# Hybrid decoder layer: the change-over between the two FFN products reordered, the last weight group loaded earlier, its last product split in two

## The chip, the cores and the metric

The kernel runs on one core of one Trainium2 chip. The metric is the time of one execution on the device in microseconds, the median of several runs. The engines are named as in the profile: PE (matrix products; PEld loads their stationary operand), DVE (vector), ACT (scalar), POOL (GpSimd) and SP (which issues DMAs).

## The reference

One decoder layer on x of 512 tokens by 2048. The token mixer (gated linear attention and differential attention) comes first and isn't touched here. The change lies in the second half, a gated MLP with a causal depthwise convolution, and its closing norm:

```python
h = rmsnorm(x, ffn_pre_norm)
up = h @ w_ffn_in                       # 2048 x (2 * 5632)
a, b = up[..., :D_FF], up[..., D_FF:]
a = conv_w[0] * a_pad[0:S] + conv_w[1] * a_pad[1:S+1] + conv_w[2] * a_pad[2:S+2] + conv_b
f = (gelu(a) * b) @ w_ffn_out           # 5632 x 2048
x = x + rmsnorm(f, ffn_post_norm)
```

## The kernel before

**Numbers and pieces.** Every fp32 operand is split into a high part (an ACT copy to the reduced fp32 type, L138 or L151) and a low part (a DVE subtraction, L139 or L152), and each product is three matmuls: high by high, high by low, low by high. A *weight half* ("granule", L129) is 128 x 1024 weights, loaded by DMA into a raw tile, split into one of three slots of the tile `ring`, or into a spare pair of tiles (`xhi`, `xlo`; from the pool tag "rt", or one pair that is kept).

**Units.** The 5632 hidden columns are 44 blocks of 128, 11 groups of four. Group 0 is done plainly (its result lies in DRAM as `ud0`); groups 1 to 10 go through a scheme of seven products instead of eight on 2 x 2 blocks (class `Unit`, L1221). A unit has the products `x0`, `z0`, `y0`, `z1`, `x1`, `y1`, `y2`, each of two weight halves, of which each takes 12 matmuls of 512 columns (down) or 24 of 256 (up). Products of one letter add up in the same PSUM banks; `x0` also opens `y`. After each product `out` reads the banks: ACT copies or DVE adds. The weights of a product are sums too: `x0` and `z1` are followed by an accumulating DMA that POOL issues (L1246, L1506) onto the raw tile, and DVE adds others (L1464, L1281). The other operand of a product (`a11`, `s5`, `s2`, `s3`, `a12`, `s7`, `a22`) is a token-block sum. For the up units it lies in `ah`, `al` and six tiles; for the down units it comes back from DRAM (`sd`) into a small tile `st` and is split into a fixed place of `ah`, `al` (`prepare`, L1389; places at L1384). Place (3, 1) belongs to no operand; (0, 0) is `a11`'s, free after the last `x0`. Small tiles (tag t4) have six buffers.

**Order.** The up units run first (20 of them, L1428), then ten down units, five pairs of groups by two halves of the 2048 output columns, each adding into `acc[t]`, one 128 x 2048 tile for each of four token tiles. Outside of blocks marked as ordered by hand, the kernel's planner orders the instructions by its own model of their times, and may move a load far ahead of its place in the text. Inside `manual_schedule(engines=IN_ORDER)` PE, ACT, DVE and POOL take the order of the text, while SP's DMAs are still placed by the planner.

**The change-over** (`change_over`, L1523) is such an ordered block: the last four products of the last up unit u (from `x1`), all of the first down unit d0 but for the end of `z` and `x`, and `x0` of d1, written as a list of products. `run_in_order` (L1487) splits weight halves two or three ahead of their product, and after each half calls the functions that `at` and `prepare_at` hung there: loads, operand splits, weight sums, the sums that u's result is stored as (`late_sums`), and the allocation of `acc` (`late_tiles`).

**The last group.** `whole` (L1670) loads the two halves of `ud0` and splits them into places (3, 1) and (0, 0). `last_group` (L1620) multiplies it by the last weights in four column blocks c of 512 for the four token tiles t: `ffn_out_part` is 12 matmuls and DVE's add into `acc` (L1608); `square` is ACT's sum of squares (L1613); `scale` multiplies by the gain (L1617); a DVE sum over the four blocks and two POOL steps (L145, L147) give the reciprocal root; `finish` is the final sum with the residual (L1637) and the store. Block 0 is ordered by the planner, blocks 1 to 3 by hand, token tile by token tile; block 3's weights are split after the first product of block 1.

Of the kernel before, what the change touches and what calls it, by code (L numbers as in the profile page):

```python
# [17 lines left out]
P = 128  # L18
# [17 lines left out]
def hybrid_layer(ctx: ExitStack, tc: tile.TileContext, x, attn_pre_norm, w_in, w_alpha_up, b_alpha,  # L36
# [10 lines left out]
    def dma(o, i):  # L47
        return nc.sync.dma_start(out=o, in_=i)
# [114 lines left out]
    def bcast_row(tile_ap, row):  # L163
        dma(tile_ap, row.partition_broadcast(P))
# [1224 lines left out]
    def prepare(c, n):  # L1389
        raw = small_tile("st")  # L1390
        dma(raw, sd[c][n].rearrange("p g x -> p (g x)"))
        split(piece(ah, *place[n]), piece(al, *place[n]), raw)
# [60 lines left out]
    def at(u, seg, g, *fs):  # L1453
        hooks.setdefault((u, seg, g), []).extend(fs)

    def load_unit(u):
        u.t = [load_t(u.block(0, 0, g), u.a) for g in range(2)]
        u.b22, u.b21 = [], []

    def load_b(u, name, i, j, by=None):  # L1460
        getattr(u, name).extend(load(u.block(i, j, g), u.a, by) for g in range(2))

    def add_t(u, name, g):
        tt(u.t[g], u.t[g], getattr(u, name)[g], ALU.add)  # L1464
# [13 lines left out]
    def prepare_at(c, n, load_at, split_at):  # L1478
        f, g = prepare_parts(c, n)
        at(*load_at, f)  # L1480
        at(*split_at, g)
# [40 lines left out]

    def change_over(u):  # L1523
        d0, d1 = downs[:2]
        order = [(u, "x1"), (d0, "x0"), (u, "y1"), (u, "y2")]
        order += [(d0, g) for g in ("z0", "y0", "z1", "x1")] + [(d1, "x0"), (d0, "y1"), (d0, "y2")]
        at(u, "x1", 1, late_tiles)
        prepare_at(0, "s2", (u, "x1", 0), (d0, "x0", 1))
        prepare_at(0, "s3", (u, "x1", 1), (u, "y1", 0))
        prepare_at(0, "s7", (u, "y1", 1), (u, "y2", 0))  # L1530
        prepare_at(0, "a12", (d0, "x0", 0), (d0, "z0", 0))
        prepare_at(0, "a22", (u, "y2", 0), (d0, "y0", 0))
        at(u, "x1", 1, lambda: (add_t(u, "b21", 0), add_t(u, "b21", 1)))
        at(u, "x1", 0, lambda: load_b(d0, "b22", 1, 1))
        at(u, "y1", 1, lambda: load_b(d0, "b21", 1, 0))
        at(d0, "z0", 1, lambda: load_unit(d1))
        for g in range(2):
            at(u, "y2", g, lambda g=g: add_t(d0, "b22", g))
        at(d0, "z1", 0, lambda: add_t(d0, "b21", 0))
        at(d0, "x1", 0, lambda: add_t(d0, "b21", 1))  # L1540
        for where in ((d0, "z0", 0), (d0, "y0", 0), (d0, "z1", 0), (d0, "x1", 0)):
            at(*where, lambda: late_sums.pop(0)())
        return order

# [5 lines left out]
        prepare(0, n)  # L1550
    with tc.manual_schedule(engines=IN_ORDER):
        run_in_order(order, lambda i: 2 if i < 10 else 3)

    extra[0] = True
    downs[1].z0(held=True)
    for i, u in enumerate(downs):
        if i == 0:
            continue
        nxt = downs[i + 1] if i + 1 < len(downs) else None
        nc_ = (i + 1) // 2  # L1560
        first = i % 2 == 0
        last_cb = i % 2 == 1 and nxt is not None

        if first:
            prepare(i // 2, "s3")
        if i == 6:
            g3 = large_tile("g3")
            bcast_row(g3, ffn_post_norm[0])
        u.y0()
        if first:  # L1570
            prepare(i // 2, "a12")
        if last_cb:
            prepare(nc_, "a11")
        u.z1()
        if first:
            prepare(i // 2, "s7")
        u.x1()
        if last_cb:
            prepare(nc_, "s5")
        if nxt is not None:  # L1580
            nxt.x0()
        if first:
            prepare(i // 2, "a22")
        u.y1()
        if last_cb:
            prepare(nc_, "s2")
        u.y2()
        if nxt is not None:
            nxt.z0()
# [2 lines left out]


    def ffn_out_weights(gi, c):
        return [granule(w_y3[:, 4 * gi + 2 * q:4 * gi + 2 * q + 2, 512 * c:512 * (c + 1)], 2,
                        spare={(3, 1): True, (2, 1): "rt", (3, 0): "rt"}.get((c, q))) for q in range(2)]

    def ffn_out_part(us, gr, t, c):
        b = bank()
# [17 lines left out]
        tt(acc[t][:, sl] if dst is None else dst, acc[t][:, sl], g3[:, sl], ALU.mult)  # L1617


    def last_group(gi, us):  # L1620
        gr = ffn_out_weights(gi, 0)
        for t in range(NT):
            ffn_out_part(us, gr, t, 0)
            square(t, 0)
            scale(t, 0)
        gr = {c: ffn_out_weights(gi, c) for c in (1, 2)}

        rs = {}
        x1 = {t: v[:, h].rearrange("p k c -> p (k c)").bitcast(F32)
              for t, (v, h) in enumerate(((ah, 1), (al, 1), (ah, 2), (al, 2)))}  # L1630
        for t in range(NT):
            dma(x1[t], x1d[t])

        def finish(t, *ps, last=None):
            for i in ps:
                sl = slice(512 * i, 512 * (i + 1))
                stt(acc[t][:, sl], last if last is not None and i == 3 else acc[t][:, sl], rs[t],  # L1637
                    x1[t][:, sl], ALU.mult, ALU.add)
                if t == 3:
                    dma(out2[t * P:(t + 1) * P, sl], acc[t][:, sl])  # L1640
                elif i % 2:
                    sl = slice(512 * i - 512, 512 * (i + 1))
                    dma(out2[t * P:(t + 1) * P, sl], acc[t][:, sl])

        with tc.manual_schedule(engines=IN_ORDER):
            end = small_tile("end")[:, :512]
            for t in range(NT):
                ffn_out_part(us, gr[1], t, 1)
                square(t, 1)
                if t == 0:  # L1650
                    gr[3] = ffn_out_weights(gi, 3)
                else:
                    finish(t - 1, 0)
                scale(t, 1)
                if t:
                    finish(t - 1, 1)
                ffn_out_part(us, gr[2], t, 2)
                square(t, 2)
                if t:
                    finish(t - 1, 2, 3)  # L1660
                ffn_out_part(us, gr[3], t, 3)
                square(t, 3)
                scale(t, 2)
                scale(t, 3, end if t == 3 else None)
                ss = small.tile([P, 1], F32, name="ss", tag="ss")
                nc.vector.reduce_sum(ss, ssf[t], axis=AX.X)
                rs[t] = rsqrt_mean(ss, D)
            finish(3, 0, 1, 2, 3, last=end)

    whole = []  # L1670
    for q, at in enumerate(((3, 1), (0, 0))):
        raw = small_tile("st")
        dma(raw, ud0[:, 2 * q:2 * q + 2, :].rearrange("p n t -> p (n t)"))
        hi, lo = (piece(v, *at) for v in (ah, al))
        split(hi, lo, raw)
        for n in range(2):
            whole.append((hi[:, S * n:S * (n + 1)], lo[:, S * n:S * (n + 1)]))
    last_group(0, whole)


# [28 lines left out]
```

## Time and profile before

| | |
|---|---|
| median of 3 runs | 2078.6 us (2077.53 to 2078.65) |
| the profiled execution | 2076.67 us, span 2075.0 us, granted PE clock 0.999 |
| PE busy | 2047.0 us, 99% |
| DVE busy | 1507.1 us, 73% |
| ACT busy | 1000.0 us, 48% |
| DMA | mean 173 GB/s |

Times inside the program are microseconds from the span's start. The up units end, and the change-over lies, about 1618 to 1660; the down units run to about 2022; the last group runs from there to the end, its last product ending near 2065. A busy PE row counts overlapping matmuls, so what a matmul costs is read from the distance of two starts. In a timeline row the bracket gives how long the engine was idle before the row, and what ended that.

### The profile page before, as it was taken

To read this page: it belongs to the slowest core of one execution; us is meant where nothing else is said; L and a number is where in the kernel's file an instruction comes from. 1 tells how busy PE (TensorE), PEld (TensorE's weight loads), DVE (VectorE), ACT (ScalarE), POOL (GpSimd) and SP (SyncE) were. 2 spreads that over 40 slices of the span, in tenths; PEclk is the share of its full clock that TensorE was granted. 3 is DMA by queue.
4 is the path that set the end of the run, shared out by engine and by line. 5 is a ranking of instruction groups with operands and counts; after the bars stand their busy time and mean duration, and the time that the engine had idled before them with its cause. 6 is when DMAs were issued, how large, how long until landed. Compare 5 with 4: busy or idle time off the path is not lost.

```text
span 2075.0 us, 35488 instructions
## 1 busy us (share of the span) xinstructions
PE 2047.0 (99%) x14417; PEld 1893.9 (91%) x14417; DVE 1507.1 (73%) x1790; ACT 1000.0 (48%) x1301; POOL 290.2 (14%) x306
## 2 busy tenths in 40 slices
PE   7999999999999999999999999999999999999998
PEld 6799999999988889899999999999999888888786
DVE  5967777666762265977777777777777888988877
ACT  5544444455652243454554554555455654444433
POOL 0112223222200000011011111111110111101100
PEclk9999999999999999999999999999999999999999
DMA  5488887878883354458667577567677896775753
GB/s 213 121 189 184 191 199 180 196 174 200 197 263 120 93 181 152 113 119 196 147 154 194 138 163 189 135 166 178 147 164 188 225 249 171 196 208 144 180 155 142
DMA packets 281465, 358.61 MB, mean 173 GB/s; under 512 B 14848, under 2 KB 223156, under 8 KB 279380
## 3 DMA queue, kind: packets, MB, share of 16 engines
q1 hardware_dynamic: 192148, 259.85, 37.3%
q0 software_dynamic: 84800, 94.38, 29.9%
q10 hardware_dynamic: 4352, 2.10, 0.4%
q8 instruction: 113, 1.85, 0.3%
q14 instruction: 52, 0.43, 0.1%
HBM read 311.72 MB, written 44.56 MB: 172 GB/s over the span
## 4 chain that ended last, share of the span: by engine, by line
PE 67%; DVE 2%; issue 1%; DMA 1%; ACT 1%; POOL 0%; DVEq 0%; POOLq 0%; SPq 0%; ACTq 0%
PE bank L1298 12%; PE bank L1299 12%; PE bank L1300 12%; PE bank L1401 6%; PE bank L1402 6%; PE bank L1400 6%; PE bank L194 3%; PE bank L193 3%; PE bank L192 3%; PE bank L176 1%; PE bank L175 1%; PE bank L174 1%; DVE ring L139 1%; PE bank L1605 0%; PE bank L1606 0%
## 5 line engine op out<-in xcount | busy, mean ns | idle before, releaser
L138 ACT ACTIVATE ring<-raw 128x1024 fp32r<-128x1024 f32 x316 | 334.7, 1061 | 494.0 <-PE bank L1299 115.6
L139 DVE TENSOR_TENSOR ring<-raw,ring 128x1024 fp32r<-128x1024 f32 x316 | 384.1, 1221 | 251.6 <-ACT ring L138 250.6
L1298 PE MATMUL bank<-ah,ring 128*128 128x256 f32 x1280 | 353.4, 276 | 1.5 <-DVE u L1331 1.5
L1300 PE MATMUL bank<-ah,ring 128*128 128x256 f32 x1280 | 353.3, 276 | 0.0
L1299 PE MATMUL bank<-al,ring 128*128 128x256 f32 x1280 | 353.3, 276 | 0.0
L138 ACT ACTIVATE ring<-rt 128x1024 fp32r<-128x1024 f32 x220 | 233.3, 1061 | 248.3 <-PE bank L1299 155.1
L139 DVE TENSOR_TENSOR ring<-rt,ring 128x1024 fp32r<-128x1024 f32 x220 | 268.5, 1222 | 90.1 <-ACT ring L138 87.1
L1298 PEld LDWEIGHTS bank<-ah,ring 128*128 128x128 f32 x1280 | 240.3, 188 | 1.7 <-ACT ring L138 1.7
L1299 PEld LDWEIGHTS bank<-al,ring 128*128 128x128 f32 x1280 | 240.3, 188 | 0.1
L1300 PEld LDWEIGHTS bank<-ah,ring 128*128 128x128 f32 x1280 | 240.3, 188 | 0.0
L1401 PE MATMUL bank<-ring,ah 128*128 128x512 f32 x424 | 165.3, 390 | 1.9 <-DVE ring L139 1.9
L1402 PE MATMUL bank<-ring,al 128*128 128x512 f32 x424 | 165.0, 389 | 0.0
L1400 PE MATMUL bank<-ring,ah 128*128 128x512 f32 x424 | 152.4, 389 | 0.0
L193 PE MATMUL bank<-ring,ah 128*128 128x512 f32 x280 | 109.6, 393 | 0.0
L192 PE MATMUL bank<-ring,ah 128*128 128x512 f32 x280 | 109.4, 396 | 0.0
L194 PE MATMUL bank<-ring,al 128*128 128x512 f32 x280 | 108.9, 392 | 0.0
L1246 POOL DMA_DIRECT2D raw<-in_w_ffn_in_dram x40 | 51.2, 1309 | 395.3 <-DVE ring L139 395.3
L1401 PEld LDWEIGHTS bank<-ring,ah 128*128 128x128 f32 x424 | 79.6, 188 | 19.3 <-DVE ring L139 2.8
L1246 POOL DMA_DIRECT2D rt<-in_w_ffn_in_dram x40 | 50.9, 1279 | 327.0 <-DVE ring L139 315.0
L1400 PEld LDWEIGHTS bank<-ring,ah 128*128 128x128 f32 x424 | 79.6, 188 | 16.6
L1402 PEld LDWEIGHTS bank<-ring,al 128*128 128x128 f32 x424 | 79.6, 188 | 16.5
L797 PE MATMUL bank<-ring,ah 128*128 128x256 f32 x320 | 91.8, 287 | 0.2 <-ACT ah L151 0.2
(358 smaller groups left out, 5646.3 us busy)
## 6 DMA issues: line engine op xcount, KB each, us to landing
raw<-in_w_ffn_in_dram SPq DMA_DIRECT2D x96, 512.0 KB, 4.7
raw<-in_w_in_dram SPq DMA_DIRECT2D x56, 512.0 KB, 4.6
raw<-in_w_ffn_out_dram SPq DMA_DIRECT2D x48, 512.0 KB, 6.2
raw<-in_w_in_dram POOLq DMA_DIRECT2D x40, 512.0 KB, 7.3
rt<-in_w_ffn_in_dram SPq DMA_DIRECT2D x40, 512.0 KB, 5.9
rt<-in_w_ffn_in_dram POOLq DMA_DIRECT2D x40, 512.0 KB, 6.1
raw<-in_w_ffn_in_dram POOLq DMA_DIRECT2D x40, 512.0 KB, 6.6
raw<-in_w_o_dram SPq DMA_DIRECT2D x32, 512.0 KB, 4.1
```

The lines of the kernel that those rows point to most:

```text
L138: act(hi, raw, AF.Copy)
L139: tt(lo, raw, hi.bitcast(F32), ALU.subtract)
L192: mm(banks[t], ah[:, t, s, :], w[0][:, k, :], start=st, stop=False)
L193: mm(banks[t], ah[:, t, s, :], w[1][:, k, :], start=False, stop=False)
L194: mm(banks[t], al[:, t, s, :], w[0][:, k, :], start=False, stop=sp)
L1246: nc.gpsimd.dma_start(out=raws[g].rearrange("p (a b) -> p a b", a=self.a), in_=self.block(0, j, g), accum_op=ALU.add)
L1298: mm(o, wh, sh[:, :, kk, :], start=start and kk == 0 and n == 0, stop=False, **NOW)
L1299: mm(o, wh, sl[:, :, kk, :], start=False, stop=False, **NOW)
L1300: mm(o, wl, sh[:, :, kk, :], start=False, stop=kk == HK - 1, **NOW)
L1400: mm(b[j], sh[:, o:o + P], w[0][:, q, :], start=start and st == 0, stop=False, **NOW)
L1401: mm(b[j], sh[:, o:o + P], w[1][:, q, :], start=False, stop=False, **NOW)
L1402: mm(b[j], sl[:, o:o + P], w[0][:, q, :], start=False, stop=st == 3, **NOW)
```

## The change

1. In the change-over the list opens with `x0` of d0, and the last up unit follows as `y1`, `x1`, `y2` (before: `x1`, `x0` of d0, `y1`, `y2`). The loads, splits, weight sums and late sums hang at other products, most of the splits and late sums later.
2. `ud0`'s two halves are loaded at the head of down unit 8 (`load_first`) and split behind the next unit's `x0` (`split_first`, the first half there, the second after the loop), in place of both after the loop.

3. In the last group, block 0 is ordered by hand too. Block 1's weights are loaded into "rt" tiles and split after block 0's first product (its second half into the kept pair); block 2's after block 0. Block 1's products for token tiles 0 and 1 come first, with block 3's weights split between them; then the order is as before.
4. The last product (token tile 3, block 3) becomes `last_block`: two halves of 256 columns on two banks, each with its add and square. DVE sums the first parts of the squares while the second half runs, and POOL takes the last add and the root. `scale` of block 2 moves ahead of it.

```diff
--- before.py
+++ after.py
@@ -1522,23 +1522,23 @@
 
     def change_over(u):
         d0, d1 = downs[:2]
-        order = [(u, "x1"), (d0, "x0"), (u, "y1"), (u, "y2")]
+        order = [(d0, "x0"), (u, "y1"), (u, "x1"), (u, "y2")]
         order += [(d0, g) for g in ("z0", "y0", "z1", "x1")] + [(d1, "x0"), (d0, "y1"), (d0, "y2")]
-        at(u, "x1", 1, late_tiles)
-        prepare_at(0, "s2", (u, "x1", 0), (d0, "x0", 1))
-        prepare_at(0, "s3", (u, "x1", 1), (u, "y1", 0))
-        prepare_at(0, "s7", (u, "y1", 1), (u, "y2", 0))
-        prepare_at(0, "a12", (d0, "x0", 0), (d0, "z0", 0))
-        prepare_at(0, "a22", (u, "y2", 0), (d0, "y0", 0))
-        at(u, "x1", 1, lambda: (add_t(u, "b21", 0), add_t(u, "b21", 1)))
-        at(u, "x1", 0, lambda: load_b(d0, "b22", 1, 1))
-        at(u, "y1", 1, lambda: load_b(d0, "b21", 1, 0))
+        at(d0, "x0", 0, lambda: load_b(d0, "b22", 1, 1))
+        at(d0, "x0", 0, late_tiles)
+        at(d0, "x0", 1, lambda: (add_t(u, "b21", 0), add_t(u, "b21", 1)))
+        at(u, "x1", 1, lambda: load_b(d0, "b21", 1, 0))
         at(d0, "z0", 1, lambda: load_unit(d1))
+        prepare_at(0, "s2", (d0, "x0", 1), (u, "y2", 0))
+        prepare_at(0, "s3", (u, "y1", 1), (d0, "z0", 0))
+        prepare_at(0, "a12", (u, "x1", 0), (d0, "z0", 1))
+        prepare_at(0, "s7", (u, "x1", 1), (d0, "y0", 1))
+        prepare_at(0, "a22", (u, "y2", 0), (d0, "z1", 1))
         for g in range(2):
             at(u, "y2", g, lambda g=g: add_t(d0, "b22", g))
         at(d0, "z1", 0, lambda: add_t(d0, "b21", 0))
         at(d0, "x1", 0, lambda: add_t(d0, "b21", 1))
-        for where in ((d0, "z0", 0), (d0, "y0", 0), (d0, "z1", 0), (d0, "x1", 0)):
+        for where in ((d0, "y0", 0), (d0, "x1", 1), (d1, "x0", 0), (d1, "x0", 1)):
             at(*where, lambda: late_sums.pop(0)())
         return order
 
@@ -1550,6 +1550,19 @@
         prepare(0, n)
     with tc.manual_schedule(engines=IN_ORDER):
         run_in_order(order, lambda i: 2 if i < 10 else 3)
+
+    whole, first_raws = [], []
+
+    def load_first():
+        for q in range(2):
+            first_raws.append(small_tile("st"))
+            dma(first_raws[q], ud0[:, 2 * q:2 * q + 2, :].rearrange("p n t -> p (n t)"))
+
+    def split_first():
+        hi, lo = (piece(v, *((3, 1), (0, 0))[len(whole) // 2]) for v in (ah, al))
+        split(hi, lo, first_raws[len(whole) // 2])
+        for n in range(2):
+            whole.append((hi[:, S * n:S * (n + 1)], lo[:, S * n:S * (n + 1)]))
 
     extra[0] = True
     downs[1].z0(held=True)
@@ -1566,6 +1579,8 @@
         if i == 6:
             g3 = large_tile("g3")
             bcast_row(g3, ffn_post_norm[0])
+        if i == 8:
+            load_first()
         u.y0()
         if first:
             prepare(i // 2, "a12")
@@ -1581,6 +1596,8 @@
             nxt.x0()
         if first:
             prepare(i // 2, "a22")
+        if i == 8:
+            split_first()
         u.y1()
         if last_cb:
             prepare(nc_, "s2")
@@ -1592,8 +1609,12 @@
 
 
     def ffn_out_weights(gi, c):
-        return [granule(w_y3[:, 4 * gi + 2 * q:4 * gi + 2 * q + 2, 512 * c:512 * (c + 1)], 2,
-                        spare={(3, 1): True, (2, 1): "rt", (3, 0): "rt"}.get((c, q))) for q in range(2)]
+        got = []
+        for q in range(2):
+            src = w_y3[:, 4 * gi + 2 * q:4 * gi + 2 * q + 2, 512 * c:512 * (c + 1)]
+            got.append(granule(src, 2, load_t(src, 2) if c == 1 else None,
+                               spare={(1, 1): True, (2, 1): "rt", (3, 0): "rt"}.get((c, q))))
+        return got
 
     def ffn_out_part(us, gr, t, c):
         b = bank()
@@ -1617,13 +1638,44 @@
         tt(acc[t][:, sl] if dst is None else dst, acc[t][:, sl], g3[:, sl], ALU.mult)
 
 
+    def last_block(us, gr):
+        tk = slice(3 * P, 4 * P)
+        both = small.tile([P, 2], F32, name="ss2", tag="ss2", bufs=4)
+        halves = [both[:, i:i + 1] for i in range(2)]
+        for h in range(2):
+            b = bank()[:, :256]
+            o = slice(256 * h, 256 * (h + 1))
+            sl = slice(1536 + 256 * h, 1536 + 256 * (h + 1))
+            for k in range(4):
+                uh, ul = us[k]
+                hi, lo = gr[k // 2]
+                mm(b, uh[:, tk], hi[:, k % 2, o], start=k == 0, stop=False)
+                mm(b, uh[:, tk], lo[:, k % 2, o], start=False, stop=False)
+                mm(b, ul[:, tk], hi[:, k % 2, o], start=False, stop=k == 3)
+            tt(acc[3][:, sl], acc[3][:, sl], b, ALU.add)
+            jk = fp.tile([P, 2, 256], F32, name="jk6", tag="p1", bufs=2)
+            act(jk[:, 0, :], acc[3][:, sl], AF.Square, scale=D ** -0.5, accum_out=halves[h])
+            if h == 0:
+                pre = small.tile([P, 1], F32, name="ss", tag="ss")
+                nc.vector.reduce_sum(pre, ssf[3][:, :3], axis=AX.X)
+                ts(pre, pre, 1.0 / D, EPS, ALU.mult, ALU.add)
+                tt(pre, pre, halves[0], ALU.add)
+        ms = small.tile([P, 1], F32, name="ms", tag="ms")
+        nc.gpsimd.tensor_tensor(ms, halves[1], pre, ALU.add)
+        r = small.tile([P, 1], F32, name="rs", tag="rs")
+        nc.gpsimd.tensor_tensor(r, ms, nhalf[:, :1], ALU.pow)
+        return r
+
     def last_group(gi, us):
-        gr = ffn_out_weights(gi, 0)
-        for t in range(NT):
-            ffn_out_part(us, gr, t, 0)
-            square(t, 0)
-            scale(t, 0)
-        gr = {c: ffn_out_weights(gi, c) for c in (1, 2)}
+        gr = {0: ffn_out_weights(gi, 0)}
+        with tc.manual_schedule(engines=IN_ORDER):
+            for t in range(NT):
+                ffn_out_part(us, gr[0], t, 0)
+                if t == 0:
+                    gr[1] = ffn_out_weights(gi, 1)
+                square(t, 0)
+                scale(t, 0)
+            gr[2] = ffn_out_weights(gi, 2)
 
         rs = {}
         x1 = {t: v[:, h].rearrange("p k c -> p (k c)").bitcast(F32)
@@ -1644,37 +1696,41 @@
 
         with tc.manual_schedule(engines=IN_ORDER):
             end = small_tile("end")[:, :512]
-            for t in range(NT):
+            for t in range(2):
                 ffn_out_part(us, gr[1], t, 1)
                 square(t, 1)
                 if t == 0:
                     gr[3] = ffn_out_weights(gi, 3)
-                else:
+                scale(t, 1)
+            for t in range(NT):
+                if t > 1:
+                    ffn_out_part(us, gr[1], t, 1)
+                    square(t, 1)
+                if t:
                     finish(t - 1, 0)
-                scale(t, 1)
+                if t > 1:
+                    scale(t, 1)
                 if t:
                     finish(t - 1, 1)
                 ffn_out_part(us, gr[2], t, 2)
                 square(t, 2)
                 if t:
                     finish(t - 1, 2, 3)
+                if t == 3:
+                    scale(t, 2)
+                    rs[t] = last_block(us, gr[3])
+                    scale(t, 3, end)
+                    break
                 ffn_out_part(us, gr[3], t, 3)
                 square(t, 3)
                 scale(t, 2)
-                scale(t, 3, end if t == 3 else None)
+                scale(t, 3)
                 ss = small.tile([P, 1], F32, name="ss", tag="ss")
                 nc.vector.reduce_sum(ss, ssf[t], axis=AX.X)
                 rs[t] = rsqrt_mean(ss, D)
             finish(3, 0, 1, 2, 3, last=end)
 
-    whole = []
-    for q, at in enumerate(((3, 1), (0, 0))):
-        raw = small_tile("st")
-        dma(raw, ud0[:, 2 * q:2 * q + 2, :].rearrange("p n t -> p (n t)"))
-        hi, lo = (piece(v, *at) for v in (ah, al))
-        split(hi, lo, raw)
-        for n in range(2):
-            whole.append((hi[:, S * n:S * (n + 1)], lo[:, S * n:S * (n + 1)]))
+    split_first()
     last_group(0, whole)
```

## The prediction

> **What bounds the kernel now.** I read the page's busy table first, then who waited for whom on PE, then busy time by stretches, and last the timelines around each wait. Line 1 is the busy table of the page; the next lines are PE's waits (total, times, longest), then one stretch (length, busy time and count of PE, PEld, DVE, ACT, POOL, granted clock, DMA share, GB/s).
>
> ```profile
> PE 2047.0 (99%) x14417; PEld 1893.9 (91%) x14417; DVE 1507.1 (73%) x1790; ACT 1000.0 (48%) x1301; POOL 290.2 (14%) x306
> ```
> ```profile
> PE bank L1401 <- DVE ring L139: 1.9, 1, 1.9
> PE bank L1298 <- DVE u L1331: 1.5, 1, 1.5
> ...
> PE bank L1605 <- DVE xlo L139: 0.8, 1, 0.8
> ```
> ```profile
> 1680.00:1900.00 220.00, 220.00 (x973) 182.15 (x972) 189.06 (x198) 109.67 (x110) 28.34 (x24) 1.00 0.72 189
> ```
>
> PE is busy end to end. The change takes away no product, so it can win only waits (these three lie where it edits) and the tail behind the last product. Everything else it can only lose. DVE is second: 189 of 220 us in the down stage, so on a stretch where work is in a fixed order it can take PE's place.
>
> **Change-over.** The last up unit u has `y1` and `y2` on one bank. In the order of before they are neighbours:
>
> ```profile
> 1634.65 0.28 PE L1299 MATMUL bank<-al,ring 128*128 128x256 f32 x1
> 1634.77 0.28 PE L1300 MATMUL bank<-ah,ring 128*128 128x256 f32 x1
> 1636.54 0.36 PE L1298 MATMUL bank<-ah,ring 128*128 128x256 f32 x1 [1.50 <-DVE u L1331]
> ```
> ```profile
> 1635.71 0.68 DVE L1331 TENSOR_TENSOR u<-u,bank 128x512 f32<-128x512 f32 x1
> ```
>
> 256-column matmuls start 0.113 us apart; here `y2` must wait until DVE has read `y1`'s result out of the bank: 1.77 - 0.11 = 1.66 us. In the new order `x1` stands between them, 48 matmuls of 0.113, 5.44 us, on another bank. The read-out needs 0.68 us and at most one 1024-wide instruction before it (1.23, below), so it is covered: **-1.66**.
>
> What is late next? `d0.x0` opens, so `u.y1` is one product earlier after `z1`, and its weights come from an accumulating transfer that POOL issues only once `z1`'s weights are read:
>
> ```profile
> 1612.96 1.28 POOL L1246 DMA_DIRECT2D raw<-in_w_ffn_in_dram  x1 [1.46 <-DVE ring L139]
> ```
> ```profile
> raw<-in_w_ffn_in_dram POOLq DMA_DIRECT2D x40, 512.0 KB, 6.6
> ```
> ```profile
> 1622.32 1.23 DVE L139 TENSOR_TENSOR ring<-rt,ring 128x1024 fp32r<-128x1024 f32 x1 [1.50 <-ACT ring L138]
> ```
>
> The second of the two transfers should land near 1619.6. The fourth weight half of the ordered stretch, now `y1`'s second, takes the turn of this subtraction, whose ACT copy begins 1.1 us before it, 1621.2. That leaves 1.6 us, and the first, a step earlier in both, as much. ACT, and DVE behind it, are in order: if a transfer is later, every later copy and split queues behind it, and PE loses what exceeds its lead of some 2 us. The moved splits, adds and late sums are the same instructions. Laying 1.13 per 1024-wide DVE step and 0.6 per 512-wide one along the new order (2.72 us a step), no step holds over 3.5 us and none comes after its product needs it; the tightest, `y0`'s first half behind two adds and the product of `y2`, has 0.7 us. The loads of `d0.b22` wait on SP for a buffer, which `y1`'s two halves now free before the adds on `b21` do; the operand loads queued on SP behind them come earlier too, and POOL's accumulations for `d0.x0` two steps, 5.4 us, earlier. So 0, bounds 0 and +2.0 (the size of the waits that the region shows).
>
> **The load of the last group's operands.** The two halves of `ud0` are loaded and split behind the loop in the text, but the planner hoisted them. From the chain of waits (start, length), ACT's and PE's timelines:
>
> ```profile
> 1928.95 8.26 DMA st<-ud
> ```
> ```profile
> 1937.23 1.06 ACT L151 ACTIVATE ah<-st 128x1024 fp32r<-128x1024 f32 x1 [3.98 <-DMA st<-ud]
> ```
> ```profile
> 1941.70 0.61 PE L1400 MATMUL bank<-ring,ah 128*128 128x512 f32 x2
> 1944.21 0.50 PE L1401 MATMUL bank<-ring,ah 128*128 128x512 f32 x1 [1.90 <-DVE ring L139]
> 1944.55 0.39 PE L1402 MATMUL bank<-ring,al 128*128 128x512 f32 x1
> ```
>
> Matmuls of 512 columns start 0.227 apart (973 in the 220 us above), so 1944.21 is 2.06 late and the next one 0.11 more: 2.17 us, because ACT stood 3.98 us before the split. PE therefore had about 1.8 us of lead. The first half goes to a place that no down product uses, so nothing but its load holds it; other splits of the loop wait for PE. Now the loads stand ahead of unit 8's last three operand loads, the first of which went out here, in a stretch whose DMA share is 0.42:
>
> ```profile
> 1900.50 0.34 SPq L48 DMA_DIRECT2D st<-sd4a  x1
> ```
> ```profile
> 1900.00:1920.00 20.00, 20.00 (x90) 16.57 (x89) 17.16 (x19) 8.55 (x9) 1.17 (x1) 1.00 0.42 109
> ```
>
> If the first half takes that buffer, it is 28 us earlier and should land sooner than 8.26. I take **-2.17**, bounds -2.17 and 0 (it stands elsewhere); the loop else has no wait to lose.
>
> **Last down unit.** Part of the last group's first product ran early, between that unit's `y1` and `y2`:
>
> ```profile
> 2014.63 0.62 PE L1604 MATMUL bank<-ring,ah 128*128 128x512 f32 x2
> ```
> ```profile
> 2013.20 1.23 DVE L139 TENSOR_TENSOR ring<-raw,ring 128x1024 fp32r<-128x1024 f32 x1 [1.49 <-ACT ring L138]
> 2014.34 1.28 DVE L1408 TENSOR_TENSOR acc<-acc,bank 128x512 f32<-128x512 f32 x2
> ```
>
> In the ordered block it can no longer be put there. `y2`'s first bank is read out at 2014.34 + 0.68, so without these twelve matmuls (2.72 us) PE would stand from 2014.63 to about 2015.1: **+0.5**, bounds 0 (DVE reads it out before the split at 2013.20) and +1.4 (both reads in turn).
>
> **Last group.** Let X be the end of column block 0's products: 36 matmuls after the row below, 2030.95.
>
> ```profile
> 2022.79 0.39 PE L1604 MATMUL bank<-ring,ah 128*128 128x512 f32 x1
> ...
> 2038.35 0.50 PE L1605 MATMUL bank<-xlo,ah 128*128 128x512 f32 x1 [0.76 <-DVE xlo L139]
> ```
> ```profile
> 2034.59 0.68 DVE L1608 TENSOR_TENSOR acc<-acc,bank 128x512 f32<-128x512 f32 x1
> 2037.07 2.36 DVE L139 TENSOR_TENSOR xlo<-raw,xhi 128x1024 fp32r<-128x1024 f32 x2 [1.80 <-ACT xhi L138]
> 2039.34 0.69 DVE L1617 TENSOR_TENSOR acc<-acc,g 128x512 f32<-128x512 f32 x1
> ```
> ```profile
> 2035.36 0.63 ACT L1613 ACTIVATE jk<-acc 128x512 f32<-128x512 f32 x1 [1.61 <-DVE acc L1608]
> ...
> 2035.99 1.99 ACT L138 ACTIVATE xhi<-raw 128x1024 fp32r<-128x1024 f32 x2
> ```
> ```profile
> 2065.65 0.69 DVE L1608 TENSOR_TENSOR acc<-acc,bank 128x512 f32<-128x512 f32 x1 [0.62 <-PE bank L1606]
> 2066.26 0.68 DVE L1617 TENSOR_TENSOR acc<-acc,g 128x512 f32<-128x512 f32 x1
> ...
> 2067.46 0.15 DVE L1666 TENSOR_REDUCE ss<-ssf 128x1 f32<-128x4 f32 x1
> 2068.55 2.07 DVE L1637 SCALAR_TENSOR_TENSOR acc<-acc,rs,al 128x512 f32<-128x512 f32 x3 [0.94 <-POOL rs L147]
> ```
>
> Before, PE's products end 0.2 before the last add, at 2065.4, 34.4 after X, and the twelve blocks of 2.72 need 32.6: PE loses 1.8 us, since blocks 1 and 3's operands come just as they are needed. A second token tile of block 1 in front gives block 3's operands 2.72 us more, so PE would lose only some 0.3 and end at X+33.0, not X+34.4. But the vector engines have the same work in a fixed order. Steps from these rows: add to square 0.77, square to next ACT copy 0.63, copy to subtraction 1.07, subtraction to next 1.13, add or scale to next 0.6, square to its scale 0.76, reduction to the first final sum 1.1, one of those to the next 0.67 (2.07 for three). Along the new order: add (tile 3, block 0) X+0.2, its square 1.0, block 2's copy 1.6, subtractions 2.7 and 3.8, add (0,1) 5.0, square 5.7, block 3's copy 6.4, subtractions 7.4 and 8.6, scale 9.7, add (1,1) 10.3, its scale 11.8, adds 12.4 and 13.0, scales 14.0 and 14.6, reduction 15.2, first final sum of tile 0 at 16.4. Before, that was 2044.50, X+13.55, with two fewer instructions done (1.2 us): the chain is 1.6 us behind. Per tile it then needs 4 x 0.67 + 6 x 0.6 + 0.25 + two waits of 0.33 = 7.2 us against PE's 8.16, so it regains what it lost without ever resting: tile 1's first final sum 23.0 after a turn of 6.6 without block 1, tile 2's 30.1, first half's add 34.5, while PE is done with that half at 31.6. DVE, not PE, sets the end.
>
> For the two halves:
>
> ```profile
> L599 ACT ACTIVATE jk<-bank 128x256 f32<-128x256 f32 x16 | 6.0, 376 | 3.6 <-PE bank L596 3.6
> L511 DVE TENSOR_TENSOR d<-gb 128x256 f32<-128x256 f32 x20 | 8.3, 417 | 2.4 <-DMA gb<-bcd 1.8 <-PE bank L595 0.6
> ```
>
> A half add is 0.42 (not 0.69), its square 0.38 (not 0.63): from add to final sum it takes 0.5 to the square, 0.5 for it and its accumulator and the 1.0 of POOL's part, 2.0 us instead of 2.9, with no scale and reduction between. But the second half's add stands on DVE behind a small sum that waits for the first half's square (0.4 + 0.1 + 0.5 + 0.1 = 1.1). So 34.5 + 1.2 + 2.0 = X+37.7; before it was 2068.55, X+37.6. The four final sums and stores are unchanged: **+0.1**, bounds -0.9 (the waits in the chain close up, and the halves give what they save) and +0.7. The matmuls cost nothing: 24 of 0.113 for 12 of 0.227, though each has its weight load:
>
> ```profile
> L1298 PEld LDWEIGHTS bank<-ah,ring 128*128 128x128 f32 x1280 | 240.3, 188 | 1.7 <-ACT ring L138 1.7
> ```
>
> On that the Trainium skill, page TensorE: Matmul & The Clock Gate, Part 3 (Packing small matmuls), speaks against the change: a weight load overlaps running matmuls only where it goes to other row groups of the array. By it the 12 further full loads would lie open. The trace disagrees: matmuls 0.113 us from start to start, each with a load of 0.188 us, cannot have their loads in the open.
>
> **Sum**, against the profiled execution (2076.67 us, span 2075.0): -1.66 - 2.17 + 0.5 + 0.1 = -3.2, so 2073.4. That execution lies 1.9 under the median of the runs; the same -3.2 on 2078.6 is **2075.4 us**. About 0.2%, 4.2 us, is what counts as a difference: this falls short of it.
>
> **Rivals.**
> 1. *Every PE wait turns into time.* For: each is in PE's own list. Against: DVE's chain above. Time: -1.66 - 2.17 - 1.8 = -5.6, 2073.0; with a 0.9 us shorter tail 2072.1. Chance 0.26.
> 2. *The wait on `ud0` stays*, because the planner again puts its split where its own model has the load landed. For: it did. Against: the earlier, emptier place. -1.1, 2077.5. Chance 0.13.
> 3. *The change-over trades its wait for one on `y1`'s accumulation or in DVE's queue.* Margins 1.6 and 0.7 us. Up to +2.0: 2077.4. Chance 0.07.
> 4. *Slower: ACT stands in front of `ud0`'s split right behind its issue.* Price: the wait less PE's 1.8 us of lead; ACT idle for a whole 8.26 us landing costs 6.5, so 2075.4 + 6.5 = 2081.9. It is slower than before once that wait passes 1.8 + 3.2 = 5.0 us. For: ACT is in order, and nothing else holds that split. Against: the DMA share of the earlier stretch, and that the wait of before, in the crowded one, was 3.98. Chance 0.09.
> 5. *Weight loads of the halves lie open*, 12 x 0.188 = 2.3 us on PE. In the forecast DVE's lag behind PE (35.7 against 33.2 at the second add) covers it; where PE sets the end, it leaves rival 1 at 2075.3. The 0.113 spacing speaks against it. Chance 0.02.
>
> **How the numbers follow.** Forecast 0.43. Faster by over 0.2% (under 2074.4): rival 1 and a quarter of the forecast's own spread (filler at 0, chain closing up), 0.37. Slower (over 2082.8): the part of rival 4 in which a landing takes a microsecond longer still or both halves of `ud0` wait, and a little of 3, 0.06. The rest 0.57. The range goes down to 2072.4, near the whole of rival 1, and up to 2078.4, over rivals 2 and 3 with a bound of the last unit added.
>
> **What would show it.** In PE's waits the row of L1331 is gone and no row over 0.3 us takes its place there; no ACT split waits on `ud`; PE stands up to 0.5 us before the last unit's `y2`. In the last group PE ends over a microsecond before DVE's add of the second half begins, and the final sums begin 37.7 us after block 0's last product. Wrong if that add waits for PE (then rival 1), or if an ACT wait on a load appears.

## The result, and the profile after

| kernel | median of 22 runs | lowest to highest |
|---|---|---|
| before | 2079.85 us | 2077.24 to 2088.84 |
| changed | 2077.0 us | 2074.40 to 2079.95 |

Ratio 0.9983, 95% interval 0.9975 to 0.9991: 0.17% faster, inside the 0.2% that was to count as no difference. The prediction had 0.9985 and "no difference" as the likeliest. The trace shows that this agreement is half luck: the sum put a stall of 2.6 us or more at 0, and two other terms came out 1.9 us lower than it had them.

The changed kernel's profiled execution took 2077.34 us, span 2075.6. Its busy line, and the one row of PE's waits that lies behind the first up product:

```profile
PE 2048.7 (99%) x14429; PEld 1896.9 (91%) x14429; DVE 1508.4 (73%) x1793; ACT 1000.0 (48%) x1303; POOL 291.9 (14%) x306
```
```profile
PE bank L1400 <- DVE acc L1408: 2.2, 1, 2.2
```

The two waits of before are gone (L1401's 1.9 and L1298's 1.5), and so is the last group's (L1605's 0.8). One that was not there has come. It begins at 1678.15, 36 us behind the end of `y2`, the last product of the up units. PE's timeline, then DVE's, then one row of SP:

```profile
1677.70 0.61 PE L1400 MATMUL bank<-ring,ah 128*128 128x512 f32 x2
1680.52 0.50 PE L1400 MATMUL bank<-ring,ah 128*128 128x512 f32 x1 [2.21 <-DVE acc L1408]
```
```profile
1667.57 0.69 DVE L1373 TENSOR_TENSOR s<-s,u 128x512 f32<-128x512 f32 x1
...
1673.55 1.23 DVE L139 TENSOR_TENSOR ring<-rt,ring 128x1024 fp32r<-128x1024 f32 x1 [1.29 <-ACT ring L138]
1678.04 0.69 DVE L1373 TENSOR_TENSOR s<-s,u 128x512 f32<-128x512 f32 x1 [3.27 <-DMA sd4s<-s]
1678.65 1.22 DVE L139 TENSOR_TENSOR xlo<-rt,xhi 128x1024 fp32r<-128x1024 f32 x1
1679.79 0.68 DVE L1408 TENSOR_TENSOR acc<-acc,bank 128x512 f32<-128x512 f32 x1
```
```profile
1668.28 0.34 SPq L48 DMA_DIRECT2D sd4s<-s  x1
```

The row at 1678.04 is the fourth late sum, `s3`. The four sums share two buffers (L1372, tag "sum"), so the fourth writes where the second, `s2` at 1667.57, still lies, and its store, issued at 1668.28, has to be done first. That takes 9.8 us, in a stretch where the DMA share is above 1. DVE stands 3.27 us, and behind it in DVE's order stands the reading out of a bank (1679.79) that PE needs. From 1677.92, the start of the second of the two matmuls in PE's first row, to the next is 2.60 us instead of 0.23: 2.37 lost.

It does not end there. Busy time by stretches, with the granted clock behind the five engines:

```profile
1680.50:1681.70 1.20, 1.18 (x5) 1.00 (x6) 1.20 (x2) 0.00 (x0) 0.00 (x0) 1.00 0.89 242
1681.70:1685.00 3.30, 3.29 (x10) 2.22 (x9) 3.30 (x4) 0.00 (x0) 0.23 (x1) 0.54 0.73 263
1685.00:1690.00 5.00, 5.00 (x23) 4.10 (x22) 3.35 (x4) 3.53 (x5) 0.94 (x1) 0.96 0.60 102
```

Some 1.5 us after PE starts again its clock falls to half, by the trace's clock records from 1681.99 to 1685.40, and matmuls of 512 columns start 0.427 us apart. Added up over the distances of starts from 1677.92 to 1686, PE loses 4.31 us: 2.37 of waiting, 1.94 of slow starts, nearly all of it half clock.

**A stretch that can be compared.** The code up to the 6001st of the 6720 up products is the same in all kernels below (PE, DVE and ACT run the same instructions in the same order), but the profiled executions reach it between 1552.8 and 1559.3. So the traces are compared from that product's start to the end of the span, called E here: 521.8 us before (1553.1 to 2075.0), 520.7 after (1554.9 to 2075.6). The forecast of -3.2 wanted 518.6. In parts: change-over -1.74 (1.66, and 0.08 of a slow first matmul), short waits near 1650 -0.19, new stall +4.31, `ud0` -2.17, last group -1.3: -1.1.

### The profile page after: what moved, and what is told of

It is laid out like the page before. It is cut to its first block, busy times and chain, and to the rows that moved or that the text cites. A ratio compares the mean times of both kernels' runs of the same rounds, so it can differ in the third digit from the quotient of the medians.

```text
span 2075.6 us, 35519 instructions
## 1 busy us (share of the span) xinstructions
PE 2048.7 (99%) x14429; PEld 1896.9 (91%) x14429; DVE 1508.4 (73%) x1793; ACT 1000.0 (48%) x1303; POOL 291.9 (14%) x306
## 4 chain that ended last, share of the span: by engine, by line
PE 93%; DVE 2%; DMA 2%; issue 1%; ACT 1%; POOL 1%; DVEq 0%; SPq 0%; POOLq 0%; ACTq 0%
PE bank L1298 12%; PE bank L1299 12%; PE bank L1300 12%; PE bank L1400 6%; PE bank L1401 6%; PE bank L1402 6%; PE bank L193 3%; PE bank L192 3%; PE bank L194 3%; PE bank L793 3%; PE bank L795 3%; PE bank L794 3%; PE bank L797 2%; PE bank L798 2%; PE bank L799 2%; PE bank L176 2%
## 5 line engine op out<-in xcount | busy, mean ns | idle before, releaser
L1298 PE MATMUL bank<-ah,ring 128*128 128x256 f32 x1280 | 354.0, 277 | 0.0
L1298 PEld LDWEIGHTS bank<-ah,ring 128*128 128x128 f32 x1280 | 240.5, 188 | 0.1
L1401 PE MATMUL bank<-ring,ah 128*128 128x512 f32 x424 | 165.7, 391 | 0.0
L1401 PEld LDWEIGHTS bank<-ring,ah 128*128 128x128 f32 x424 | 79.9, 188 | 16.4
```

The lines of the kernel that those rows point to most:

```text
L1298: mm(o, wh, sh[:, :, kk, :], start=start and kk == 0 and n == 0, stop=False, **NOW)
L1401: mm(b[j], sh[:, o:o + P], w[1][:, q, :], start=False, stop=False, **NOW)
```

## The experiments

E is from each run's profile; ratios go against runs of the kernel before on the same chip (medians there 2079.2 to 2079.3).

| run | median us | ratio [95%] | E us |
|---|---|---|---|
| third_sum_in_place | 2071.95 | 0.9964 [0.9952, 0.9976] | 516.4 |
| changeover_alone | 2079.6 | 1.0000 [0.9992, 1.0009] | 522.4 |
| load_alone | 2077.14 | 0.9988 [0.9980, 0.9997] | 519.7 |
| group_alone | 2077.9 | 0.9997 [0.9988, 1.0005] | 522.4 |
| sums_old_steps | 2072.9 | 0.9971 [0.9960, 0.9983] | 516.9 |
| sums_closer | 2078.16 | 0.9993 [0.9984, 1.0001] | 521.4 |
| whole_last_product | 2072.43 | 0.9967 [0.9954, 0.9980] | 515.8 |
| small_sum_later | 2072.03 | 0.9969 [0.9958, 0.9980] | 515.8 |
| scales_behind | 2072.92 | 0.9967 [0.9954, 0.9979] | 515.6 |
| before, again (two) | 2079.42, 2077.88 | | 521.6, 521.7 |
| changed, again | 2078.56 | | 519.0 |

### Is it the sum's buffer?

```diff
-                t = made[n] = fp.tile([P, 2, 256], F32, name=n, tag="sum", bufs=2)
+                t = made[n] = y if (gi, n) == (NG - 1, "s3") else fp.tile([P, 2, 256], F32, name=n, tag="sum", bufs=2)
```

> The changed kernel, with one line other: the fourth of the last up unit's sums (s3) is written over its own operand a12, whose store left long before, instead of into the buffer that the second sum (s2) filled 10.4 us earlier and whose store is still under way. Theory A (that buffer is all of the new stall): DVE waits for no store of sd4 behind the change-over, PE has no wait over 0.3 us between the change-over and the last group, no matmul in that stretch stands at 0.427 us, and the changed stretches are 4.3 us shorter than in the changed kernel's profiled execution: a median near 2073, ratio to before 0.996 to 0.998. Rival B (the transfers, with a DMA share of 1.04 there, hand over the operands too late in any case): PE waits over 1 us in the same 15 us for an operand's split, and the time stays within 1.5 us of the changed kernel's, 2076 to 2078.

Its DVE timeline at the same place, and its stretches from the change-over to the last group:

```profile
1665.39 0.68 DVE L1373 TENSOR_TENSOR s<-s,u 128x512 f32<-128x512 f32 x1
...
1668.87 0.68 DVE L1373 TENSOR_TENSOR u<-s,u 128x512 f32<-128x512 f32 x1
1669.47 1.21 DVE L152 TENSOR_TENSOR al<-st,ah 128x1024 fp32r<-128x1024 f32 x1
1670.60 1.22 DVE L139 TENSOR_TENSOR xlo<-rt,xhi 128x1024 fp32r<-128x1024 f32 x1
```
```profile
1630.00:1660.00 30.00, 30.00 (x178) 26.39 (x177) 25.98 (x25) 19.58 (x23) 3.57 (x3) 1.00 0.76 219
1660.00:1700.00 40.00, 40.00 (x179) 33.10 (x177) 35.34 (x36) 23.25 (x27) 5.65 (x6) 1.00 0.92 260
1700.00:2010.00 310.00, 310.00 (x1369) 256.71 (x1368) 268.98 (x285) 146.39 (x142) 35.75 (x31) 1.00 0.69 184
```

Theory A holds, rival B falls. The fourth sum runs 3.5 us behind the second and waits for nothing; PE is busy 380 of 380 us and the clock stays whole. E is 4.3 below the changed kernel's, the price counted above, and 5.4 below the one before: -1.74 - 0.19 - 2.17 - 1.3. This kernel is faster than both; its interval and the changed kernel's just overlap (0.9976 and 0.9975).

Two runs move the sums instead:

```diff
-        for where in ((d0, "y0", 0), (d0, "x1", 1), (d1, "x0", 0), (d1, "x0", 1)):
+        for where in ((d0, "z0", 0), (d0, "y0", 0), (d0, "z1", 0), (d0, "x1", 0)):    # sums_old_steps
+        for where in ((d0, "y0", 0), (d0, "x1", 1), (d1, "x0", 0), (d1, "x0", 0)):    # sums_closer
```

> The changed kernel with the four late sums of the last up unit on the steps that they had before (behind d0's z0, y0, z1 and x1, first halves), all else as changed. Theory A: the second and the fourth sum are then four steps of 2.72 us apart, 10.9 us, about as long as the second one's store holds its buffer (10.4), so DVE waits for the store under 1.6 us and PE under 0.3: the new stall and its half-rate matmuls go, 2.4 to 4.3 us less than the changed kernel, ratio to before 0.996 to 0.998. Rival: the sums, now between the splits that d0's first products need, delay these instead, and PE loses 0.6 us or more at y0.

> The changed kernel with the fourth late sum one step of 2.72 us earlier, right behind the third: the wait on the store is made longer. Theory A: DVE stands some 6 us instead of 3.3, PE some 5 instead of 2.4, so 2.6 us more than the changed kernel, ratio to before about 0.9995. On the clock: if the half-rate stretch behind a wait of PE has one length (3 us, 1.9 lost), it costs nothing more; if it grows with the wait, 2 us more, ratio 1.0005. Rival B (the stall is not the store's): no difference to the changed kernel.

DVE's rows of the second and fourth sum in the first, then the fourth in the second:

```profile
1652.80 0.69 DVE L1373 TENSOR_TENSOR s<-s,u 128x512 f32<-128x512 f32 x1
...
1665.81 0.68 DVE L1373 TENSOR_TENSOR s<-s,u 128x512 f32<-128x512 f32 x1
```
```profile
1678.21 0.69 DVE L1373 TENSOR_TENSOR s<-s,u 128x512 f32<-128x512 f32 x1 [3.14 <-DMA sd4s<-s]
```

On their old steps the two sums are 13.0 us apart, no wait is left, and the new order of products keeps its gain: it was the steps of the sums, not the moved product, that cost. (E is 0.5 more than with the sum in place: PE starts 0.22 and 0.11 us late at 1658.6 and 1659.1, a small part of what the rival said.) In the other run the expected 6 us did not come: the store's end sets when the fourth sum runs, so asking a step earlier doesn't add a step. What changed is what stands behind it on DVE: one more 1024-wide subtraction, so PE waited 3.38 instead of 2.37. The half clock behind it cost 1.75, about as before: its length does not grow with the wait.

### The parts alone

The three edits, each put into the kernel before by itself; the diffs are those of the change, split in three.

> The kernel before with the new order of the change-over alone. By the prediction's term (one wait gone, none new): -1.7 us, ratio 0.9992. By theory A: the wait before y2 is gone (-1.7), and DVE stands some 3 us before the fourth sum, for which PE pays 2.4 us and, where the clock drops behind it, 4.3: +0.7 to +2.6 us, ratio 1.0003 to 1.0013.

> The kernel before with the load and split of ud0 inside the loop alone. Prediction's term: PE's 2.17 us in front of the late matmuls of 1941.7 go, and no other wait comes: -2.2 us, ratio 0.9990. Rival (the split stands behind its load elsewhere, ACT waits over 5 us there and PE pays): no gain or a loss.

> The kernel before with the last group alone in its new order and its last product in halves; ud0 is loaded behind the loop as before. Prediction's terms: +0.5 before the last down unit's y2 and +0.1 at the end. By the changed kernel's trace: no wait before y2, and from block 0's last product to the end 42.7 us where it was 44.0: -1.3 us, ratio 0.9994. Rival: PE's 1.8 us of waits all turn into time, and the halves give 0.9 more: -2.7 us, 0.9987.

PE's waits of the change-over alone:

```profile
PE bank L1400 <- DVE acc L1408: 2.2, 1, 2.2
PE bank L1401 <- DVE ring L139: 1.6, 1, 1.6
```

It brings the stall with it (2.41 us), and `ud0`'s wait stays, as it must: +0.6 of E and no change in time. The load alone is the part that gains: -1.9 to -2.1 of E against the three profiles of the kernel before, and no PE wait over 0.2 us in the loop of the down units. ACT still waits for the first half, 3.74 us here and 3.54 us in the changed kernel, whose row follows, and PE pays nothing:

```profile
1909.88 1.06 ACT L151 ACTIVATE ah<-st 128x1024 fp32r<-128x1024 f32 x1 [3.54 <-DMA st<-ud]
```

The last group alone shows +0.6 of E, for a reason that lies outside the group: behind the `ud0` wait, here 1.95 us, the clock fell to half.

```profile
1952.00:1954.00 2.00, 2.00 (x6) 1.57 (x5) 2.00 (x3) 0.00 (x0) 0.00 (x0) 0.50 0.34 125
```

From block 0's last product (X) to the end it takes 42.75 us, as in the changed kernel (42.7), against 44.0 before: -1.3.

### What the halves bring

The changed kernel's DVE rows: the add and the subtractions that open the hand-made order, tile 0's first final sum, and the last product with its final sums. X is 2032.92.

```profile
2033.12 0.69 DVE L1629 TENSOR_TENSOR acc<-acc,bank 128x512 f32<-128x512 f32 x1 [0.38 <-PE bank L1627]
...
2035.61 1.23 DVE L139 TENSOR_TENSOR ring<-raw,ring 128x1024 fp32r<-128x1024 f32 x1 [0.26 <-ACT ring L138]
2036.75 0.68 DVE L1629 TENSOR_TENSOR acc<-acc,bank 128x512 f32<-128x512 f32 x1
2037.35 1.22 DVE L139 TENSOR_TENSOR xlo<-raw,xhi 128x1024 fp32r<-128x1024 f32 x1
...
2048.11 1.42 DVE L1689 SCALAR_TENSOR_TENSOR acc<-acc,rs,ah 128x512 f32<-128x512 f32 x2 [0.96 <-POOL rs L147]
...
2066.16 0.41 DVE L1655 TENSOR_TENSOR acc<-acc,bank 128x256 f32<-128x256 f32 x1
...
2067.20 0.16 DVE L1662 TENSOR_TENSOR ss<-ss,ss 128x1 f32<-128x1 f32 x1 [0.38 <-ACT jk L1657]
2067.28 0.41 DVE L1655 TENSOR_TENSOR acc<-acc,bank 128x256 f32<-128x256 f32 x1
...
2069.22 2.08 DVE L1689 SCALAR_TENSOR_TENSOR acc<-acc,rs,al 128x512 f32<-128x512 f32 x3 [0.81 <-POOL rs L1666]
```

The second half's add comes 1.12 behind the first's, held by the small sum of 2067.20, which waits for ACT. Three runs on top of the sum in place take this apart: the last product whole again; the small sum (L1659 to L1662) moved out of the loop, behind the second add; and with that `scale(t, 2)` moved behind `last_block`.

```diff
                 if t == 3:
-                    scale(t, 2)
                     rs[t] = last_block(us, gr[3])
+                    scale(t, 2)
                     scale(t, 3, end)
```

> The kernel with the fourth sum written in place, and the last product of the last group whole again (one add, one square, the usual reduction). By the changed kernel's trace the first half's add begins 33.2 us after block 0's last product (X) and the final sums at X+36.3; a whole add at 33.2 plus the 2.9 us from add to final sum of the kernel before gives X+36.1: the halves bring nothing, within 0.3 us either way, ratio that of the kernel with the sum in place. Rival: the halves bring 0.9 us, final sums at X+37.2.

> The kernel with the fourth sum written in place, and the small sum over the first half's square (with the two small instructions before it) moved behind the second half's add on DVE. If DVE's order in front of that add sets the end: the add follows the first half's at 0.4 instead of 1.1 us, final sums at X+35.6 instead of 36.3, -0.7 us. Rival: ACT's two squares in a row or POOL's part set it, and the final sums stay at X+36.3.

> The kernel with the sum in place and the small sum later, and in addition the scaling of tile 3's block 2 moved behind the two half adds. If the halves' gain is held back by DVE's work in front of their adds: the second half's add then begins right behind PE's last product, X+33.1, and with 2.25 us from there to the final sums these begin at X+35.35, 0.4 sooner than with the last product whole (X+35.74). Rival (the two scalings and the small instructions no longer fit beside square and power): final sums at X+35.8 as before this edit. Either way 0.02%, seen in the trace and not in the times.

One fence each, the add or adds and the first of the final sums (X is 2029.99, 2028.13 and 2031.96):

```profile
2062.83 0.69 DVE L1629 TENSOR_TENSOR acc<-acc,bank 128x512 f32<-128x512 f32 x1
...
2065.73 2.08 DVE L1689 SCALAR_TENSOR_TENSOR acc<-acc,rs,al 128x512 f32<-128x512 f32 x3 [0.95 <-POOL rs L147]
```
```profile
2061.36 0.74 DVE L1655 TENSOR_TENSOR acc<-acc,bank 128x256 f32<-128x256 f32 x2
...
2063.93 2.08 DVE L1689 SCALAR_TENSOR_TENSOR acc<-acc,rs,al 128x512 f32<-128x512 f32 x3 [0.71 <-POOL rs L1666]
```
```profile
2064.60 0.78 DVE L1655 TENSOR_TENSOR acc<-acc,bank 128x256 f32<-128x256 f32 x2
...
2067.53 2.08 DVE L1689 SCALAR_TENSOR_TENSOR acc<-acc,rs,al 128x512 f32<-128x512 f32 x3 [0.44 <-POOL rs L1666]
```

The final sums begin at X+36.3 in the changed kernel, +35.74 with the product whole, +35.80 with the small sum later and +35.57 with the scaling behind too. Six profiles with the last group as built have it between X+36.28 and X+36.32, so these steps are larger than the spread. As built, the halves cost 0.6 us, and moving the small sum alone wins 0.5 of it back (expected 0.7). Expected was no difference for the whole product; the whole one's add came at X+32.84, 0.4 sooner than reckoned, because `scale(t, 2)` no longer stood in front of it. At best the halves give 0.2 us over the whole product (expected 0.4); in the times none of this shows. The halves also cost PE a little: their 24 matmuls start 0.120 us apart and not 0.113, and PE's last product ends at X+32.79 instead of X+32.64. The 2.3 us of rival 5, weight loads in the open, did not come.

### Both kernels profiled again

> The kernel before, profiled once more. Its first profiled execution took 2076.67 us, the median of its runs is 2079.2. If the clock sometimes drops behind its 2 us wait for ud0's split (as it did in the run of the last group alone, and did not in the first profile), one of the two repeats should show half-rate matmuls there and be 1.6 us or more longer from the first up product to the end (1201.8 us in the first). Rival: the difference lies in the code ahead of the first up product, and this stretch has 1201.8 each time.

> The same once more, as in the expectation of the first repeat.

> The changed kernel, profiled once more. Theory A: DVE stands about 3 us before the fourth late sum, with a release 10 us behind the second sum, and PE 2.4 us, with or without a stretch of half-rate matmuls behind it (1200.7 us from the first up product to the end with, 1198.8 without). Rival: the wait was of that one execution, and the stretch takes 1196.4.

For the kernel before, the expected cause falls: its `ud0` wait was 1.59 and 1.36 us, no half clock followed, and E is the same within 0.3 us. The first repeat's 2.75 us over the first profile lie in unchanged code: 2.2 ahead of the first up product, 0.8 behind it, -0.2 in E. For the changed kernel the stall recurs (DVE 3.03 us, PE 2.14) without half clock, and E is 519.0. From the first up product to the end it took 1201.4 us and not the 1198.8 expected; 2.3 us of that lie ahead of the 6001st up product, where nothing was changed.

## Why the prediction was right in its number, and where it was wrong

**Change-over, the wait removed (-1.66): right.** -1.74 with the slow first matmul; L1331's reading out lies far ahead of `y2`.

**"So 0, bounds 0 and +2.0" for what is late next: wrong, and the largest miss.** The step that failed is "The moved splits, adds and late sums are the same instructions": DVE's queue was laid out by durations and by when its results are needed, but not by what each instruction itself waits for. The row was there in the profile before, DVE's second and fourth sum:

```profile
1653.95 0.68 DVE L1373 TENSOR_TENSOR s<-s,u 128x512 f32<-128x512 f32 x1
...
1664.84 0.69 DVE L1373 TENSOR_TENSOR s<-s,u 128x512 f32<-128x512 f32 x1 [1.59 <-DMA sd4s<-s]
```

Before, too, the fourth sum ran 10.9 us behind the second, and only when the store let it; with four steps of 2.72 between them DVE had to wait 1.6 and PE nothing. The change leaves two steps between them; without the wait the two sums would stand 7.2 us apart (10.5 from start to start, less 3.27). The price was 2.6 to 2.9 us without half clock (the repeat: 2.14, and 0.46 of slow starts; the change-over alone: 2.41 and 0.46) and 4.3 with it; both lie beyond the bound of +2.0, which came from the waits that the region had, not from a resource. This is rival 3 in kind (a wait in DVE's queue), at a higher price and for a cause that it did not name.

**`y1`'s accumulation, margin 1.6: the margin was overrun, the price 0 was right.** POOL's, ACT's and DVE's rows for `y1`'s second half:

```profile
1614.76 1.28 POOL L1246 DMA_DIRECT2D raw<-in_w_ffn_in_dram  x1 [1.46 <-DVE ring L139]
```
```profile
1624.52 1.06 ACT L138 ACTIVATE ring<-raw 128x1024 fp32r<-128x1024 f32 x1 [3.15 <-DMA raw<-in_w_ffn_in_dram]
```
```profile
1625.61 1.23 DVE L139 TENSOR_TENSOR ring<-raw,ring 128x1024 fp32r<-128x1024 f32 x1 [2.99 <-ACT ring L138]
```

The transfer took 9.8 us and not the median of 6.6, and ACT stood 3.15 us for it, twice the margin. `d0.x0` began at 1620.22 and `y1`'s second half 24 matmuls of 0.227 and 24 of 0.113 later, at 1628.4; the subtraction ended at 1626.84. PE's lead paid for all of it, with 1.5 us to spare.

**`ud0` (-2.17): right, for a partly wrong reason.** PE's wait went. But "no ACT split waits on `ud`" was to be the sign, and ACT does wait 3.54 us in the new place. An ACT wait on a load was also named as a sign that the forecast is wrong, and it is the front end of rival 4. By rival 4's price (the wait less 1.8 us of lead) PE should have paid 1.7 us; it paid nothing, so the lead in the new place was larger than the 1.8 us that the prediction took over from the old one.

**Last down unit (+0.5): wrong, 0.** "In the ordered block it can no longer be put there": it was. Half of the filler, six matmuls, ran between `y1` and `y2`, and PE did not stop:

```profile
2016.60 0.39 PE L1625 MATMUL bank<-ring,ah 128*128 128x512 f32 x1
...
2017.73 0.39 PE L1627 MATMUL bank<-ring,al 128*128 128x512 f32 x1
2017.96 0.39 PE L1400 MATMUL bank<-ring,ah 128*128 128x512 f32 x1
```

**Last group (+0.1): the mechanism right, the size off by 1.4.** DVE and not PE sets the end, and PE is done over a microsecond before the last add, as forecast. The step that failed is in the chain, "subtractions 2.7 and 3.8, add (0,1) 5.0". The add stood between the two subtractions, at X+3.8 (2036.75). It belongs to the second ordered block and the subtraction behind it (2037.35) to the first: as with the filler above, an ordered block keeps the order inside it but is no fence towards its neighbours, and the prediction took it for one in both places. The earlier add put its square and block 3's copies, and with them all that follows, 1.2 us sooner. From there each term held: tile 0's first final sum X+15.2 (forecast 16.4), the first half's add 33.2 (34.5), the final sums 36.3 (37.7); even the 1.2 of the second add behind the small sum, measured 1.12.

**The sum.** Forecast -3.2. The terms measured, -1.74, -0.19, +2.6 to +4.3, -2.17, 0, -1.3, make -2.8 to -1.1. The times' -2.85 (interval -5.2 to -1.9) fits the end without half clock; how many of the timed runs had it is not known. Missing the stall by 2.6 or more and the last group and filler by 1.9 left the number nearly right, and that is luck: the forecast's set of steps, which had a chance of 0.43, did not come as a set.

## What to carry to other kernels

When instructions on an in-order engine are hung elsewhere, list for each not only its duration and its deadline but also the buffer that it writes and who still reads it: the distance to the last writer must exceed the store's time in that stretch (here 10 us for 256 KB), not the usual one. A small wait for a DMA that costs nothing in the profile before is such a distance used up. And where a product is halved to shorten a tail, nothing may stand between the halves that waits for the first one's result.

## What the runs showed of the hardware that was not expected

A wait of PE can cost nearly twice its length, because the clock may halve behind it. In the down stage's traces PE waits of 1.36, 1.59, 1.73, 2.06, 2.14 and 2.41 us left the granted clock whole; 1.95, 2.37 and 3.38 us were followed by 3.41 us at 0.5, worth 1.6 to 1.9 us. So near 2 us the length alone does not decide.

The clock records of the same traces show what else does. The changed kernel's clock first rises at 16.29 us; its later changes, at 1681.99, 1685.40 and 2071.11, stand 488, 489 and 602 steps of 3.413 us behind that, and in all fourteen traces the changes lie on such a grid. Laid on the grid, the three waits with a fall have 1.95, 1.94 and 3.28 us within one step, and the clock falls at that step's end, 0.1 to 1.5 us after PE has resumed. The six without a fall have at most 1.78 us in one step: the 2.06 splits into 1.78 and 0.27, the 2.41 into 1.32 and 1.09, the 2.14 into 1.29 and 0.85. So what fits all nine is how much of a wait lies within one step, and where a wait falls on the grid differs from one execution to the next. The border is not sharp by this measure: behind the changed kernel's last product 2.0 us of a step went by without a fall at its end. This was read off the traces afterwards; no run placed a wait on purpose. The Trainium skill, page TensorE: Matmul & The Clock Gate, Part 1 (The HAM clock gate), puts the fall to half rate behind an idle window of about 3.4 us, free-running, and the return after a busy window as long; the grid and the 3.41 us at half clock agree with that. That 1.94 us of waiting within such a window were enough does not fit an idle window of 3.4 us, and here the measurement decides.

What stays open: how much of a step PE must stand for the clock to fall, and why the kernel with the sum in place gained 7.3 us in the times (interval 5 to 10) where E shows 5.4; the difference is within the interval.
